# Inverse of the delta rule's triangular blocks: doubling block sizes on TensorE instead of substitution on VectorE

## The chip, the cores and the metric

One core of one Trainium2 chip runs the whole program. The metric is the device time of one execution in microseconds (us). TensorE (PE) multiplies matrices into PSUM, VectorE (DVE), ScalarE (ACT) and GpSimd (POOL) work beside it, and SyncE (SP) issues most of the DMAs.

## The reference, cut to what matters

Two transformer blocks follow each other over 1024 positions of width 1024. The second has, beside a state space model and an MLP, the delta rule of RWKV-7 with 8 heads of width 64:

```python
def step(state, inp):
    r_t, w_t, k_t, v_t, kk_t, b_t = inp
    sk = jnp.einsum('bhvk,bhk->bhv', state, kk_t)
    state = (state * w_t[:, :, None, :]
             - sk[..., None] * b_t[:, :, None, :]
             + v_t[..., None] * k_t[:, :, None, :])
    return state, jnp.einsum('bhvk,bhk->bhv', state, r_t)
```

The kernel does not step through 1024 positions. It takes them in chunks of 64, in which the steps become products of matrices; for that it needs, for each head and chunk, the inverse of a unit triangular 64x64 matrix. The change is about how that inverse is formed.

## The kernel before, in words

The 1024 positions are two halves (h = 0, 1) of four tiles of 128 positions; `rwkv(tt)` (L1226) does one tile, which is two chunks of 64 positions for 8 heads, so 16 triangular matrices. Chunk c lies on partitions 64c to 64c+63. The eight calls come from `sequences` (L923), four in a row per half, and the state links each tile to the next.

Within a tile: the masked products `MM` are made (L1328; `MM[:, h, c, 0]` holds the strictly triangular part); a block of 32x32 of each is copied to `ltc` (L1333), written to DRAM as `lt_d` (L1335, four DMAs) and read back as `L` (L1337, one DMA that repeats it over four groups of partitions), so that each partition holds a block of its own. Then VectorE substitutes in 31 steps of two instructions (L1387, L1389). The result `T` goes to DRAM as `tt_d` (L1391, four DMAs) and comes back as the diagonal blocks of `TT` (L1396, four DMAs). The off-diagonal 32x32 blocks take a transpose on VectorE (L1401), 16 small products (L1405), a copy on ScalarE (L1407), 16 more products (L1411) and two copies (L1415). `TT` is then used by L1422. The steps between L1339 and L1379 (transposes, `PQ`, `XV`, `TBK`, `W`, `G1`) don't need `TT`.

All matrix products of `rwkv` are float32 and show as two PE instructions each (16 products are x32). The large projections use split operands and three products each (`mm3`, L63; lines L66, L68, L69), one PE instruction of 512 columns each.

Order: each engine has a static order. A planner places the instructions when the kernel is built, by a model of their durations, with the order of the code as priority; steps under `urgent` come first. `sequences` writes the four tiles ahead of the projections `in2` of columns 1792 (h = 0) or 2304 (h = 1) to 4352 (L944), and the MLP follows: `ffn` of the first block's second half after h = 0 (L1090), seven of eight blocks of the second block's MLP after h = 1 (L1104). The planner puts these projections between the steps of the tiles. Their sums leave PSUM through VectorE (L902) or ScalarE (L881, L900, L1166), and their weights are loaded by SP, cast by ScalarE (L116) and split by GpSimd (L118). After h = 1, `merge_in` (L1776) reads what the tiles wrote.

The small products use the PSUM pool `tp` with four buffers in a ring; the projections use the pool `mm` with four.

Of the kernel before, what the change touches and what calls it, by code (L numbers as in the profile page):

```python
# [8 lines left out]
F32 = mybir.dt.float32  # L9
# [5 lines left out]
OP = mybir.AluOpType  # L15
# [4 lines left out]
S = 1024  # L20
D = 1024
HALF = 512
P = 128
# [11 lines left out]
class Kernel:  # L35
# [1134 lines left out]
    def rwkv_setup(self):  # L1170
        nc, I = self.nc, self.I
        c = self.rkc = self.pool("rkc")
        self.stp = self.pool("stp", 2)
        self.lora = c.tile([P, 512], F32, name="lora")
        nc.sync.dma_start(self.lora[0:64], I["w_decay_up_2"][0])
        nc.sync.dma_start(self.lora[64:128], I["w_aaa_up_2"][0])
        self.wgu = c.tile([P, 512], F32, name="wgu")
        nc.sync.dma_start(self.wgu, I["w_gate_up_2"][0])

        self.reset = c.tile([P, P], F32, name="reset")  # L1180
        nc.vector.memset(self.reset, 1.0)
        nc.vector.memset(self.reset.rearrange("p (c t) -> p c t", t=64)[:, :, 0:1], 0.0)

        self.mask2 = c.tile([P, 2, 64], F32, name="mask2")
        nc.gpsimd.memset(self.mask2, 1.0)
        for ch in range(2):
            q = self.mask2[64 * ch:64 * ch + 64]
            for m in range(2):
                nc.gpsimd.affine_select(q[:, m, :], q[:, m, :], pattern=[[1, 64]],
                                        compare_op=OP.is_gt if m == 0 else OP.is_ge, fill=0.0, base=0,  # L1190
                                        channel_multiplier=-1)

        self.ind = c.tile([P, 4, 8], F32, name="ind")
        nc.gpsimd.memset(self.ind, 0.0)
        self.blk = c.tile([P, P], F32, name="blk")
        nc.gpsimd.memset(self.blk, 0.0)
        for e in range(2):
            r = slice(64 * e, 64 * e + 64)
            nc.gpsimd.memset(self.blk[r, r], 1.0)
            for kt in range(4):  # L1200
                nc.gpsimd.memset(self.ind[r, kt, 2 * kt + e:2 * kt + e + 1], 1.0)

        self.eye2 = c.tile([P, 64], F32, name="eye2")
        nc.vector.tensor_copy(self.eye2[0:64], self.ident[0:64, 0:64])
        nc.vector.tensor_copy(self.eye2[64:128], self.ident[64:128, 64:128])

        self.eye32 = c.tile([P, 8, 32], F32, name="eye32")
        nc.gpsimd.memset(self.eye32, 0.0)
        for g in range(4):
            nc.gpsimd.affine_select(self.eye32[32 * g:32 * g + 32], self.eye32[32 * g:32 * g + 32],  # L1210
                                    pattern=[[-4, 8], [1, 32]], compare_op=OP.not_equal, fill=-1.0, base=-g,
                                    channel_multiplier=0)
        self.state = self.stp.tile([P, 4, 64], F32, name="state")
        nc.vector.memset(self.state, 0.0)
        self.lt_d = [self.dram.tile([32, 32, 32], F32, name=f"lt_d{t}") for t in range(8)]
        self.tt_d = [self.dram.tile([32, 8, 4, 32], F32, name=f"tt_d{t}") for t in range(8)]

    def rwkv_pools(self, st):
        self.rk = self.pool("rk", st=st)
        self.ew = self.pool("ew", 4, st=st)  # L1220
        self.TT = self.rk.tile([P, 8, P], F32, name="TT")
        self.nc.vector.memset(self.TT, 0.0)
        self.TI = self.rk.tile([P, 8, 32], F32, name="TI")
        self.nc.vector.memset(self.TI, 0.0)

    def rwkv(self, tt):  # L1226
        nc = self.nc
        rk = self.rk
        h, tok = tt // 4, slice(tt % 4 * P, tt % 4 * P + P)
        C = math.exp(-0.5)  # L1230
        V = nc.vector

        def big(name):
            return rk.tile([P, 4, P], F32, name=name)
# [10 lines left out]
        def ps512():  # L1245
            return self.tp.tile([P, 512], F32, name="tp")
# [7 lines left out]
        def pair(i):  # L1254
            return slice(64 * (i % 2), 64 * (i % 2) + 64), slice(i // 2 * 64, i // 2 * 64 + 64)

        chunks = [(c, slice(64 * c, 64 * c + 64)) for c in range(2)]
# [11 lines left out]
        for kt in range(4):  # L1269
            f = slice(kt * P, kt * P + P)  # L1270
            nc.tensor.matmul(pw[:, f], self.lora[0:64, f], zw[0:64, 0, :], start=True, stop=True)
            nc.tensor.matmul(pa[:, f], self.lora[64:128, f], zw[64:128, 0, :], start=True, stop=True)
        sg, a = big("sg"), big("a")
        for kt in range(4):
            f = slice(kt * P, kt * P + P)
            nc.scalar.activation(sg[:, kt, :], pw[:, f], AF.Sigmoid, bias=self.w0[:, kt:kt + 1])
        for kt in range(4):
            f = slice(kt * P, kt * P + P)
# [41 lines left out]
        MM = rk.tile([P, 8, 2, 2, 64], F32, name="MM")  # L1320
        for hh in range(0, 8, 2):
            for e in range(2):
                r = slice(64 * e, 64 * e + 64)
                ps = ps512()[:, :256].rearrange("p (c a i) -> p c a i", c=2, a=2)
# [2 lines left out]
                                     PR[r, :, hh // 2, 64 * c:64 * c + 64], start=True, stop=True)  # L1327
                V.tensor_tensor(MM[:, hh + e], ps, self.mask2[:, None].to_broadcast([P, 2, 2, 64]), op=OP.mult)  # L1328

        lt = rk.tile([P, 8, 32], F32, name="ltc")  # L1330
        for b in range(4):
            r = slice(32 * b, 32 * b + 32)
            V.tensor_copy(lt[r], MM[r, :, b // 2, 0, 32 * (b % 2):32 * (b % 2) + 32])  # L1333
        for b in range(4):
            nc.sync.dma_start(self.lt_d[tt][8 * b:8 * b + 8].rearrange("h j i -> j h i"), lt[32 * b:32 * b + 32])  # L1335
        L = rk.tile([P, 32, 32], F32, name="L")
        nc.sync.dma_start(L, self.lt_d[tt].rearrange("b j i -> b (j i)")[None].to_broadcast([4, 32, 1024]))  # L1337

        PQ = rk.tile([P, 8, 2, 64], F32, name="PQ")  # L1339
        XV = rk.tile([P, 2, 8, 64], F32, name="XV")  # L1340
# [1 line left out]
        ps = ps512()  # L1342
# [3 lines left out]
        ps = ps512()  # L1346
        for kt in range(4):
            self.transpose(ps[:, kt * P:kt * P + P], zv[:, kt, :])
        for c in range(2):
            r = slice(64 - 64 * c, 128 - 64 * c)  # L1350
            nc.scalar.copy(XV[r, c], ps[r].rearrange("p (h d) -> p h d", h=8))
        for c in range(2):
            ps = ps512()
# [6 lines left out]
        for i in range(8):  # L1360
            for c in range(2):
                r = slice(64 - 64 * c, 128 - 64 * c)
                nc.tensor.matmul(pq[64 * c:64 * c + 64, i * 64:i * 64 + 64], MM[r, i, c, 0, :], XV[r, c, i, :],
                                 start=True, stop=True)
# [4 lines left out]
        for kt in range(4):  # L1369
            f = slice(kt * P, kt * P + P)  # L1370
# [7 lines left out]
        V.tensor_tensor(W, W, k4(pg), op=OP.mult)  # L1378
        V.tensor_tensor(G1, k4(pg), bc(self.lnw), op=OP.mult)  # L1379

        T = rk.tile([P, 8, 32], F32, name="T")
        tmp = rk.tile([P, 8, 32], F32, name="Ttmp")
        nc.gpsimd.tensor_copy(T, self.eye32)
        for j in range(31):
            n = j // 4 + 1
            w = 31 - j
            V.tensor_tensor(tmp[:, :n, :w], L[:, j:j + 1, j + 1:].to_broadcast([P, n, w]),  # L1387
                            T[:, :n, j:j + 1].to_broadcast([P, n, w]), op=OP.mult)
            V.tensor_tensor(T[:, :n, j + 1:], T[:, :n, j + 1:], tmp[:, :n, :w], op=OP.subtract)  # L1389
        for cg in range(4):  # L1390
            nc.sync.dma_start(self.tt_d[tt][:, :, cg, :], T[32 * cg:32 * cg + 32])  # L1391
        TT, TI = self.TT, self.TI
        for c in range(2):
            nc.gpsimd.memset(TT[64 * c:64 * c + 32, :, 64 * c + 32:64 * c + 64], 0.0)
        for r in range(4):
            nc.sync.dma_start(TT[32 * r:32 * r + 32, :, 32 * r:32 * r + 32],  # L1396
                              self.tt_d[tt][8 * r:8 * r + 8].rearrange("h m g i -> (m g) h i"))

        for c in range(2):
            r = slice(64 * c, 64 * c + 32)  # L1400
            V.transpose(TI[r], TT[r, :, 64 * c:64 * c + 32])  # L1401
        pz = ps512()
        for i in range(8):
            for c, q in chunks:
                nc.tensor.matmul(pz[q, i * 32:i * 32 + 32], MM[q, i, c, 0, :], TI[q, i, :], start=True, stop=True)  # L1405
        Z = rk.tile([P, 8, 32], F32, name="Z")
        nc.scalar.copy(Z, pz[:, :256].rearrange("p (h j) -> p h j", h=8))  # L1407
        po = ps512()
        for i in range(8):
            for c, q in chunks:  # L1410
                nc.tensor.matmul(po[64 * c:64 * c + 32, i * 32:i * 32 + 32], Z[q, i, :], TT[q, i, 64 * c + 32:64 * c + 64],  # L1411
                                 start=True, stop=True)
        for c in range(2):
            r = slice(64 * c, 64 * c + 32)
            nc.scalar.copy(TT[r, :, 64 * c + 32:64 * c + 64], po[r, :256].rearrange("p (h i) -> p h i", h=8))  # L1415

        X = rk.tile([P, 8, 64], F32, name="X")
        for hg in range(2):
# [7 lines left out]
            for c in range(2):  # L1426
                q = slice(64 * c, 64 * c + 64)
# [5 lines left out]
        for i in range(8):  # L1433
            r, o = pair(i)
# [5 lines left out]
        for i in range(8):  # L1440
            r, o = pair(i)
# [6 lines left out]
        for c, q in chunks:  # L1448
            for i in range(8):
                r, o = pair(i)  # L1450
# [10 lines left out]
        for c, q in chunks:  # L1461
            for i in range(8):
                r, o = pair(i)
# [4 lines left out]
            pst = ps512()  # L1468
            for i in range(8):
                r = slice(64 * (i % 2), 64 * (i % 2) + 64)  # L1470
                nc.tensor.matmul(pst[r, i // 2 * 64:i // 2 * 64 + 64], FT[r, i // 2, q], self.state[r, i // 2, :],
                                 start=True, stop=True)
# [17 lines left out]
        r = self.rstd(var, 8, 1.0 / 64, 64e-5, rk)  # L1490
        V.tensor_tensor(y, y, r[:, :, None].to_broadcast([P, 8, 64]), op=OP.mult)
        po = ps512()
# [378 lines left out]
```

## Time and profile before

| what | value |
|---|---|
| median of 3 runs | 3047.42 us |
| lowest and highest of them | 3038.46, 3047.6 us |
| profiled execution, time | 3063.16 us |
| profiled execution, span of the records | 3061.4 us |
| PE busy in the span | 2831.0 us (92%) |
| DVE, ACT, POOL busy | 1745.7, 1245.3, 1460.9 us |
| the four tiles of h = 0 | about 1160 to 1655 us of the span |
| the four tiles of h = 1 | about 2010 to 2520 us of the span |

The profile gives busy time per engine, the waits of an engine with the instruction that ended them, a timeline of instructions, and the granted TensorE clock (1.00 is 2.4 GHz, 0.50 is 1.2 GHz). A group of PE instructions has its first start and a modelled length that overlaps the next group; the distance from its start to the start of the next one is what it occupies.

### The profile page before, as it was taken

How to read it: one execution, taken by the hardware profiler on the slowest of the kernel's cores; microseconds unless marked ns; L12 is line 12 of the kernel's file. 1: busy time of each engine (PE TensorE's matmuls, PEld its weight loads, DVE VectorE, ACT ScalarE, POOL GpSimd, SP SyncE). 2: the span in 40 equal slices, each digit the busy share in tenths (PEclk: the TensorE clock that was granted, in tenths of full speed). 3: DMA queues.
4: the chain of work that ended last, by engine and by line, in shares of the span. 5: the costliest groups of instructions: out<-in, count | busy, mean ns of one | idle time of the engine just before them, and what ended most of it. 6: DMA issues, size and time to landing. Idle time of an engine off the chain costs nothing.

```text
span 3061.4 us, 42378 instructions
## 1 busy us (share of the span) xinstructions
PE 2831.0 (92%) x15600; PEld 2337.1 (76%) x15600; DVE 1745.7 (57%) x3752; ACT 1245.3 (41%) x2121; POOL 1460.9 (48%) x1285
## 2 busy tenths in 40 slices
PE   6977998999998899889989999998899999999998
PEld 5865776787887777667777888887777778888887
DVE  5699569999946944445563563433655634332122
ACT  4545555444455333343333443332433333433333
POOL 4665544544445743434433465443343435454444
PEclk9988999999999999899999999999999999999999
DMA  7445332222224555333225484653323235442232
GB/s 252 136 130 178 124 118 64 90 79 69 73 84 148 179 164 152 103 86 90 76 84 147 147 274 123 178 147 107 81 92 90 82 90 155 141 131 97 97 97 83
DMA packets 301504, 370.22 MB, mean 121 GB/s; under 512 B 70936, under 2 KB 209902, under 8 KB 301040
## 3 DMA queue, kind: packets, MB, share of 16 engines
q1 hardware_dynamic: 293296, 351.75, 37.9%
q10 hardware_dynamic: 8000, 15.76, 1.5%
q8 instruction: 123, 2.02, 0.3%
q14 instruction: 85, 0.70, 0.1%
HBM read 315.80 MB, written 51.65 MB: 120 GB/s over the span
## 4 chain that ended last, share of the span: by engine, by line
PE 57%; DVE 27%; DMA 8%; issue 3%; ACT 2%; SPq 2%; POOL 1%; ACTq 0%; POOLq 0%; DVEq 0%
PE mm L66 16%; PE mm L68 16%; PE mm L69 16%; DVE junk L669 4%; DMA L<-lt_d 3%; DVE T L1389 2%; DVE Ttmp L1387 2%; DVE topk L680 2%; PE tp L128 1%; DVE acc L902 1%; DVE score L643 1%; DVE p L746 1%; DMA TT<-tt_d 1%; DVE p L735 1%; PE tp L764 1%
## 5 line engine op out<-in xcount | busy, mean ns | idle before, releaser
L118 POOL TENSOR_TENSOR whl<-wraw,whl 128x512 fp32r<-128x512 f32 (+1 forms) x836 | 1134.7, 1382 | 1255.7 <-ACT whl L116 1187.1
L66 PE MATMUL mm<-hT,whl 128*128 128x512 f32 x1760 | 699.1, 398 | 21.6 <-DVE acc L902 13.5
L68 PE MATMUL mm<-hT,whl 128*128 128x512 f32 x1760 | 701.6, 400 | 0.0
L69 PE MATMUL mm<-hT,whl 128*128 128x512 f32 x1760 | 694.8, 397 | 3.9 <-POOL whl L118 3.9
L116 ACT CAST whl<-wraw 128x1024 fp32r<-128x1024 f32 (+1 forms) x418 | 435.1, 1042 | 541.5 <-PE mm L69 389.7
L66 PE MATMUL mm<-whl,hT 128*128 128x512 f32 (+1 forms) x1584 | 614.6, 402 | 42.9 <-DVE acc L902 18.5
L68 PE MATMUL mm<-whl,hT 128*128 128x512 f32 (+1 forms) x1584 | 625.6, 396 | 0.4 <-POOL whl L118 0.4
L69 PE MATMUL mm<-whl,hT 128*128 128x512 f32 (+1 forms) x1584 | 614.3, 396 | 0.9 <-DVE hT L61 0.9
L66 PEld LDWEIGHTS mm<-hT,whl 128*128 128x128 f32 x1760 | 336.1, 191 | 97.2 <-DVE acc L902 15.2
L69 PEld LDWEIGHTS mm<-hT,whl 128*128 128x128 f32 x1760 | 336.3, 191 | 73.7 <-POOL whl L118 5.0
L66 PEld LDWEIGHTS mm<-whl,hT 128*128 128x128 f32 x1584 | 305.2, 193 | 112.2 <-DVE acc L902 22.2
L68 PEld LDWEIGHTS mm<-hT,whl 128*128 128x128 f32 x1760 | 336.1, 191 | 66.3 <-issue 0.9
L68 PEld LDWEIGHTS mm<-whl,hT 128*128 128x128 f32 x1584 | 305.9, 193 | 60.7 <-issue 1.2
L69 PEld LDWEIGHTS mm<-whl,hT 128*128 128x128 f32 x1584 | 303.3, 192 | 62.2 <-DVE hT L61 1.8
L902 DVE TENSOR_TENSOR acc<-mm,acc 128x512 f32<-128x512 f32 x240 | 160.6, 686 | 189.2 <-PE mm L69 188.7
L61 DVE TENSOR_TENSOR hT<-sm,hT 128x512 fp32r<-128x512 f32 x112 | 94.4, 846 | 265.2 <-ACT hT L60 264.5
L881 ACT ACTIVATE sm<-mm 128x512 f32<-128x512 f32 x128 | 76.5, 598 | 273.1 <-PE mm L69 267.3
L669 DVE TENSOR_SCALAR_CACHE_REDUCE junk<-score,topk 128x640 uint8<-128x640 f32 (+4 forms) x192 | 179.5, 941 | 1.8
L1387 DVE TENSOR_TENSOR Ttmp<-L,T 128x60 f32<-128x60 f32 (+24 forms) x248 | 77.8, 314 | 95.5 <-DMA L<-lt_d 88.1
L60 ACT CAST hT<-sm 128x512 fp32r<-128x512 f32 x144 | 89.3, 620 | 31.0 <-DVE sm L1835 28.3
L764 PE MATMUL tp<-pT,vhl 128*128 128x256 f32 x288 | 64.1, 310 | 25.0 <-ACT pT L760 7.4
L743 ACT ACTIVATE p<-p,nm 128x128 f32<-128x128 f32 (+7 forms) x64 | 49.6, 778 | 91.4 <-DVE nm L739 60.5
(470 smaller groups left out, 3489.2 us busy)
## 6 DMA issues: line engine op xcount, KB each, us to landing
wraw<-w_ff SPq DMA_DIRECT2D x128, 512.0 KB
wraw<-w_in SPq DMA_DIRECT2D x100, 512.0 KB
wraw<-w_ff_up SPq DMA_DIRECT2D x64, 512.0 KB
wraw<-w_ff_down SPq DMA_DIRECT2D x64, 512.0 KB
wraw<-w_ada SPq DMA_DIRECT2D x32, 512.0 KB
wraw<-w_out SPq DMA_DIRECT2D x32, 512.0 KB
raw<-w_ada SPq DMA_DIRECT2D x16, 512.0 KB
x_d<-acc ACTq DMA_DIRECT2D x16, 512.0 KB
```

The costliest lines, as they stand in the source:

```text
L60: self.nc.scalar.copy(hi, src)
L61: (engine or self.nc.gpsimd).tensor_tensor(lo, src, hi.bitcast(F32), op=OP.subtract)
L66: nc.tensor.matmul(ps, a[0], b[0], start=start, stop=False)
L68: nc.tensor.matmul(ps, a[0], b[1], start=False, stop=False)
L69: nc.tensor.matmul(ps, a[1], b[0], start=False, stop=stop)
L116: nc.scalar.copy(hl[:, 0], raw)
L118: nc.gpsimd.tensor_tensor(hl[:, 1, s], raw[:, s], hl[:, 0, s].bitcast(F32), op=OP.subtract)
L669: V.tensor_scalar(junk[:, :n], sel, value, 0.0, op0=op, op1=OP.add, accum_out=cnt)
L764: nc.tensor.matmul(o, self.vhl[(s0 + i) // 4][:, (s0 + i) % 4, kv, :], t[:, x, 256 * i:256 * i + 256], start=(s0 + i + x == 0), stop=(s0 + ...
L881: nc.scalar.activation(r, ps, AF.Relu)
L902: nc.vector.tensor_tensor(d, pss[j], d, op=OP.add)
L1387: V.tensor_tensor(tmp[:, :n, :w], L[:, j:j + 1, j + 1:].to_broadcast([P, n, w]), T[:, :n, j:j + 1].to_broadcast([P, n, w]), op=OP.mult)
```

## The change

Setup builds seven masks `joins` of 64x64 (six block patterns of width 2 to 64, and one of the neighbours above the diagonal) instead of `eye32`. In each tile, the copy to `ltc`, both trips through DRAM, the 62 instructions of the substitution, the transpose and the 32 products of 32 columns go. In their place: the identity is subtracted from the triangular blocks of `MM`, one group of 16 products of 64x64x64 (`each`) transposes them, masks start `S` and `St` at blocks of two, and five rounds double the block size. A round is a group of 16 products, a masked multiply on VectorE, two more groups (one in the last round) and two copies on ScalarE (in the last round two copies of half the partitions into `TT`).

```diff
@@ rwkv_setup
-        self.eye32 = c.tile([P, 8, 32], F32, name="eye32")
-        nc.gpsimd.memset(self.eye32, 0.0)
-        for g in range(4):
-            nc.gpsimd.affine_select(self.eye32[32 * g:32 * g + 32], self.eye32[32 * g:32 * g + 32],
-                                    pattern=[[-4, 8], [1, 32]], compare_op=OP.not_equal, fill=-1.0, base=-g,
-                                    channel_multiplier=0)
+        self.joins = c.tile([P, 7, 64], F32, name="joins")
+        nc.gpsimd.memset(self.joins, 0.0)
+        for ch in range(2):
+            q = self.joins[64 * ch:64 * ch + 64]
+            for x in range(6):
+                w = 1 << x
+                low = q[:, x].rearrange("p (b u) -> p b u", u=2 * w)[:, :, :w]
+                nc.gpsimd.memset(low, 1.0)
+                n = 32 // w
+                nc.gpsimd.affine_select(low, low, pattern=[[-2 * w, n], [0, w]], compare_op=OP.is_ge, fill=0.0, base=-w,
+                                        channel_multiplier=1)
+                nc.gpsimd.affine_select(low, low, pattern=[[2 * w, n], [0, w]], compare_op=OP.is_ge, fill=0.0,
+                                        base=2 * w - 1, channel_multiplier=-1)
+            up = q[:, 6].rearrange("p (b u) -> p b u", u=2)[:, :, 1:2]
+            nc.gpsimd.affine_select(up, up, pattern=[[-2, 32], [0, 1]], compare_op=OP.not_equal, fill=1.0, base=0,
+                                    channel_multiplier=1)
+        nc.vector.tensor_tensor(self.joins, self.joins, self.eye2[:, None].to_broadcast([P, 7, 64]), op=OP.add)
...
@@ rwkv, after MM
-        lt = rk.tile([P, 8, 32], F32, name="ltc")
-        for b in range(4):
-            r = slice(32 * b, 32 * b + 32)
-            V.tensor_copy(lt[r], MM[r, :, b // 2, 0, 32 * (b % 2):32 * (b % 2) + 32])
-        for b in range(4):
-            nc.sync.dma_start(self.lt_d[tt][8 * b:8 * b + 8].rearrange("h j i -> j h i"), lt[32 * b:32 * b + 32])
-        L = rk.tile([P, 32, 32], F32, name="L")
-        nc.sync.dma_start(L, self.lt_d[tt].rearrange("b j i -> b (j i)")[None].to_broadcast([4, 32, 1024]))
+        S, St, Y = (rk.tile([P, 8, 64], F32, name=n) for n in ("S", "St", "Y"))
+
+        def join(x):
+            return self.joins[:, x, None, :].to_broadcast([P, 8, 64])
+
+        def each(ps, a, b):
+
+            for i in range(8):
+                for c, q in chunks:
+                    nc.tensor.matmul(ps[q, i * 64:i * 64 + 64], a[c][q, i], b[q, i], start=True, stop=True)
+
+        M = [MM[:, :, c, 0, :] for c in range(2)]
+        eye = self.eye2[:, None, :].to_broadcast([P, 8, 64])
+        for c, q in chunks:
+            V.tensor_tensor(M[c][q], M[c][q], eye[q], op=OP.subtract)
+        for c, q in chunks:
+            V.tensor_tensor(St[q], M[c][q], join(6)[q], op=OP.mult)
+        ps = ps512()
+        each(ps, M, eye)
+        V.tensor_tensor(S, ps.rearrange("p (h d) -> p h d", h=8), join(0), op=OP.mult)
@@ rwkv, after W and G1
-        T = rk.tile([P, 8, 32], F32, name="T")
-        tmp = rk.tile([P, 8, 32], F32, name="Ttmp")
-        nc.gpsimd.tensor_copy(T, self.eye32)
-        for j in range(31):
-            n = j // 4 + 1
-            w = 31 - j
-            V.tensor_tensor(tmp[:, :n, :w], L[:, j:j + 1, j + 1:].to_broadcast([P, n, w]),
-                            T[:, :n, j:j + 1].to_broadcast([P, n, w]), op=OP.mult)
-            V.tensor_tensor(T[:, :n, j + 1:], T[:, :n, j + 1:], tmp[:, :n, :w], op=OP.subtract)
...
+        TT = self.TT
+        for x in range(1, 6):
+            ps = ps512()
+            each(ps, M, S)
+            V.tensor_tensor(Y, ps.rearrange("p (h d) -> p h d", h=8), join(x), op=OP.mult)
+            ps, pst = ps512(), ps512()
+            each(pst, (Y, Y), St)
+            pst = pst.rearrange("p (h d) -> p h d", h=8)
+            if x < 5:
+                each(ps, (St, St), Y)
+                nc.scalar.copy(S, ps.rearrange("p (h d) -> p h d", h=8))
+                nc.scalar.copy(St, pst)
+            else:
+                for c, q in chunks:
+                    nc.scalar.copy(TT[q, :, q], pst[q])
```

The lines left out of the second part are those from the DMAs to `tt_d` (L1390) to the copies into `TT` (L1415), which go with it; the two clears of `TT` on GpSimd (L1394) go too.

## Rows read from the trace of the kernel before

**Rows 1.** The page, part 1: busy time by engine, share of the span, instructions.
```profile
PE 2831.0 (92%) x15600; PEld 2337.1 (76%) x15600; DVE 1745.7 (57%) x3752; ACT 1245.3 (41%) x2121; POOL 1460.9 (48%) x1285
```

**Rows 2.** A window of one tile: busy PE, PEld, DVE, ACT, POOL; clock; DMA.
```profile
1282.00:1400.00 118.00, 107.00 (x762) 86.34 (x763) 61.50 (x137) 50.67 (x85) 46.33 (x38) 0.94 0.28 77
```

**Rows 3.** The chain that ended last, within the first tile: start us, us, what.
```profile
1194.25 1.43 DVE MM L1328 x4
...
1257.94 1.78 PE tp L1422 x16
```

**Rows 4.** Waits of PE, whole span: us in total, times, longest.
```profile
PE tp L1405 <- DVE TI L1401: 42.7, 8, 9.5
...
PE tp L1271 <- ACT zw L1266: 6.5, 1, 6.5
...
PE mm L66 <- ACT whl L116: 5.8, 4, 3.5
```

**Rows 5.** Waits of PE for L902, first in 1160 to 1660, then 2010 to 2520.
```profile
PE mm L66 <- DVE acc L902: 14.0, 2, 7.6
...
PE mm L66 <- DVE acc L902: 13.5, 3, 6.4
```

**Rows 6.** Timeline 1436 to 1466 (start, us, what, idle before): DVE twice, then PE.
```profile
1451.26 0.19 DVE L1387 TENSOR_TENSOR Ttmp<-L,T 128x31 f32<-128x31 f32 x1 [10.20 <-DMA L<-lt_d]
...
1457.31 0.68 DVE L902 TENSOR_TENSOR acc<-mm,acc 128x512 f32<-128x512 f32 x1
...
1458.05 0.79 PE L66 MATMUL mm<-whl,hT 128*128 128x512 f32 x1 [6.31 <-DVE acc L902]
```

**Rows 7.** Windows after the first gap, and the first and last of eight stretches.
```profile
1242.00:1245.00 3.00, 2.60 (x33) 2.44 (x34) 0.69 (x2) 0.28 (x1) 1.84 (x2) 0.50 0.86 271
...
1220.00:1260.00 40.00, 30.52 (x182) 25.03 (x182) 14.45 (x48) 9.58 (x15) 12.76 (x12) 0.83 0.45 133
...
2420.00:2480.00 60.00, 50.39 (x289) 40.56 (x287) 30.10 (x81) 16.77 (x26) 17.48 (x14) 0.89 0.31 86
```

**Rows 8.** Timeline of PE, 1608 to 1616: the two groups that go, and projections.
```profile
1608.36 1.49 PE L1405 MATMUL tp<-TI,MM 64*64 64x32 f32 x32 [1.47 <-DVE TI L1401]
1609.78 0.50 PE L66 MATMUL mm<-hT,whl 128*128 128x512 f32 x1
...
1614.77 0.70 PE L1411 MATMUL tp<-TT,Z 64*32 64x32 f32 x32
1615.39 0.50 PE L66 MATMUL mm<-hT,whl 128*128 128x512 f32 x1
```

**Rows 9.** Timeline of PE, 1203 to 1205.
```profile
1203.51 1.15 PE L1363 MATMUL tp<-XV,MM 64*64 64x64 f32 x32
1204.59 1.16 PE L1371 MATMUL tp<-zw,wgu 128*128 128x128 f32 x8
```

**Rows 10.** Timeline of PE, 1262 to 1265.
```profile
1262.98 0.39 PE L66 MATMUL mm<-hT,whl 128*128 128x512 f32 x1
1263.30 0.69 PE L1436 MATMUL tp<-MM,X 64*64 64x64 f32 x32
1263.82 0.65 PE L1443 MATMUL tp<-TBK,X 64*64 64x64 f32 x32
1264.39 0.50 PE L68 MATMUL mm<-hT,whl 128*128 128x512 f32 x1
1264.73 0.39 PE L69 MATMUL mm<-hT,whl 128*128 128x512 f32 x1
1264.96 0.40 PE L66 MATMUL mm<-hT,whl 128*128 128x512 f32 x1
```

**Rows 11.** A copy out of PSUM on ACT, 1160 to 1660: busy us, mean ns, idle before.
```profile
L1365 ACT COPY PQ<-tp 128x512 f32<-128x512 f32 x4 | 2.3, 586 | 13.0 <-PE tp L1363 13.0
```

**Rows 12.** The line of the old mask on POOL: ns min/median/max, starts.
```profile
L1210 POOL TENSOR_SCALAR_AFFINE_SELECT eye<-eye x4: 436/438/443, 981.9 to 983.3; 32x256 f32<-32x256 f32 x4
```

**Rows 13.** Groups by line on PE, 2010 to 2520 (one of six lines of projections).
```profile
L66 PE MATMUL mm<-hT,whl 128*128 128x512 f32 x342 | 138.4, 407 | 14.3 <-DVE acc L902 13.5 <-DVE hT L343 0.8
```

More of the change, by code (lines that the diff above doesn't have):

```diff
@@ L1205, in rwkv_setup @@
         nc.vector.tensor_copy(self.eye2[64:128], self.ident[64:128, 64:128])
-        self.eye32 = c.tile([P, 8, 32], F32, name="eye32")
-        nc.gpsimd.memset(self.eye32, 0.0)
-        for g in range(4):
-            nc.gpsimd.affine_select(self.eye32[32 * g:32 * g + 32], self.eye32[32 * g:32 * g + 32],
-                                    pattern=[[-4, 8], [1, 32]], compare_op=OP.not_equal, fill=-1.0, base=-g,
-                                    channel_multiplier=0)
+        self.joins = c.tile([P, 7, 64], F32, name="joins")
[15 more added lines that the diff above has]
+        nc.vector.tensor_tensor(self.joins, self.joins, self.eye2[:, None].to_broadcast([P, 7, 64]), op=OP.add)
         self.state = self.stp.tile([P, 4, 64], F32, name="state")
         nc.vector.memset(self.state, 0.0)
-        self.lt_d = [self.dram.tile([32, 32, 32], F32, name=f"lt_d{t}") for t in range(8)]
-        self.tt_d = [self.dram.tile([32, 8, 4, 32], F32, name=f"tt_d{t}") for t in range(8)]
     def rwkv_pools(self, st):
@@ L1222, in rwkv_pools @@
         self.nc.vector.memset(self.TT, 0.0)
-        self.TI = self.rk.tile([P, 8, 32], F32, name="TI")
-        self.nc.vector.memset(self.TI, 0.0)
     def rwkv(self, tt):
@@ L1390, in rwkv @@
[L1390 to L1412, printed above, removed]
@@ L1413, in rwkv @@
-        for c in range(2):
-            r = slice(64 * c, 64 * c + 32)
-            nc.scalar.copy(TT[r, :, 64 * c + 32:64 * c + 64], po[r, :256].rearrange("p (h i) -> p h i", h=8))
+        TT = self.TT
[13 more added lines that the diff above has]
+                    nc.scalar.copy(TT[q, :, q], pst[q])
```

## The prediction, made before the changed kernel was run

> **What bounds the kernel now.** I read the page first, then windows of about a tile each. PE is busy for 2831.0 us, 92% of the span [rows 1], and also while the tiles of the delta rule run: 107.00 of 118 us in the second one, for example [rows 2]. Projections that don't depend on the tile fill PE between its steps, so the chain of a tile (62 us from the end of the masks at 1195.68 to L1422 at 1257.94 [rows 3]) is mostly covered. What a tile costs is therefore PE's own work, PE's gaps, and time at the low clock. So I count these three.
>
> The waits of PE come next. Eight times, once per tile, PE stands at L1405 until the blocks are back from DRAM: 42.7 us in all [rows 4]. Five more gaps inside the tiles wait for L902, an addition on DVE that has nothing to do with the delta rule: 14.0 + 13.5 = 27.5 us [rows 5]. The timeline shows why. DVE stood 10.20 us at the first substitution, waiting for the DMA of L, with L902 behind it in its queue; L902 came at 1457.31, and PE went on 0.74 us later after 6.31 us idle [rows 6]. The same picture, DVE at L1387 and then L902, precedes the other four. By contrast the other hand-overs of a tile (PE to DVE or ACT and back, about twelve per tile) cost PE almost nothing: over all eight tiles L1271 with 6.5 us is the largest [rows 4].
>
> Third, the clock. In the first gap the granted clock fell to 0.50, and it was still there when PE worked again, 2.60 of 3 us from 1242 to 1245 [rows 7]. A level of 0.50 is 1.2 GHz, 1.00 is 2.4 GHz.
>
> **The change, part by part.** The sum is made against the profiled execution, 3063.16 us, which is 15.7 us (0.5%) above the median of 3047.42.
>
> *Added on PE.* A tile gets 1 group of 16 products at the start, 3 in each of four rounds and 2 in the last: 15, so 120 in eight tiles. The price of a group is the term that decides. L1363 has the same 16 products of 64x64x64, alternating between two diagonally opposite quarters of the array, and occupies 1204.59 - 1203.51 = 1.08 us [rows 9]. L1436, with the same shapes and count over four quarters, occupies 0.52 us [rows 10]. L1405 runs over the same two quarters as the new groups with half the columns and occupies 1.42 us, partly because its second chunk came late [rows 8]. The new code alternates chunk 0 (rows and columns 0 to 63) with chunk 1 (64 to 127), as L1363 alternates two; I take 1.08 and keep 0.52 and 1.42 as ends. 120 x 1.08 = +129.6 us (62 to 170).
>
> L1405 has half the moving columns of L1363 but is not faster [rows 8, 9], so the loading of weights seems to set the pace. The Trainium skill, page "TensorE: Matmul & The Clock Gate", section "LDWEIGHTS (loading the stationary operand)", prices a load by its columns alone, 64/1.2 = 53 ns here; an estimate from it, 32 loads one after the other, is 1.7 us per group, 205 us for 120, and the sum would end near +107 us instead of mine. The trace disagrees with that use of the rule: 1.08 us for 32 products is 34 ns each, so the loads of two quarters overlap.
>
> *Entering and leaving.* Between projections of 0.23 us each (1264.96 - 1264.73), L1436 starts 0.09 us late (1262.98 + 0.23 = 1263.21, start 1263.30), and the first projection behind the groups takes 0.34 instead of 0.23 us, 0.11 more [rows 10]. That is 0.2 us per insertion. A tile has 11 insertions (start, two per round) instead of 2 (L1405, L1411): 9 x 0.2 x 8 = +14.4 us (0, if groups stand next to other small products, to 25 at twice the price).
>
> *Removed on PE.* L1405 at 1.42 and L1411 at 0.62 us [rows 8]: 8 x 2.04 = -16.3 us.
>
> *Gaps.* With no DMA in the chain, the gaps at L1405 and behind the substitution go: -42.7 - 27.5 = -70.2 us. What is late next is the new chain's own hand-overs, 11 a tile, 88 in all. I cost them at nothing, because the twelve of the same kind cost nothing [rows 4]: the projections cover them. If the cover is thin, half a microsecond each would be 44 us.
>
> *Clock.* Eight stretches, one per tile, hold these gaps. In the first, 40 us at 0.83 lose 40 x 0.17 = 6.8 us; in the last 60 x 0.11 = 6.6 [rows 7]; the eight add to 46.4. A part of that fell while PE stood idle and is already counted; windows of 2 us over the tiles put 29.5 us on working time outside the first tile's start. -29.5 us (20 to 40).
>
> *VectorE.* The 62 steps of a tile go, and 4 copies. Ten instructions of about 0.68 us come (two subtractions, two masks for St, six masked multiplies out of PSUM, of L902's size) [rows 6]: 6.8 us. DVE gets emptier. The new wait on DVE is for a group of products; L902 and the splits of projections are queued behind it. PE comes to such groups in the planned order, as it does to L1363 or L1422 now, whose evacuations hold up no projection [rows 4, 5]. Zero.
>
> *ScalarE.* Ten copies of 0.59 us [rows 11], 5.9 us a tile, against three shorter ones that go. ACT is busy for 50.67 of 118 us in a tile [rows 2]; PE waits for them only if the fill is short. Zero, inside the hand-overs above.
>
> *DMAs and SP.* 13 DMAs a tile go from SP's queue, with their waits; weight loads stood behind them. In the whole span PE waits only 5.8 us for weights that ACT casts [rows 4], so zero. *PSUM:* 16 turns of the ring of four instead of 2; each buffer is freed by the very step for which the chain waits. Zero.
>
> *Setup.* POOL gets 12 small clears, 26 selections and a clear instead of five instructions. The old selections took 0.44 us each [rows 12]. At 0.2 to 0.4 us each some 9 us more on POOL; half of it I put on the path: +4 us (0 to 9).
>
> Sum: 129.6 + 14.4 - 16.3 - 70.2 - 29.5 + 4 = +32 us. 3063 becomes 3095 in a profiled execution, the median 3047.4 becomes 3079, given as **3080**.
>
> *Is there still enough fill?* Before, 1601 projections lay in 2010 to 2520 (342, 342, 341 and three times 192; the first of the six lines in [rows 13]). By the code, 384 of in2 and 1344 of seven MLP blocks are to be had: 1728, or 393 us at 0.23. A hand-over takes about 5 us now (L1405 ended 1609.78, L1411 began 1614.77 [rows 8]). The new chain is then 3 us of DVE, 15 groups (16 us) and 11 x 5 = 55 us: 74 instead of 62 us, so a tile grows by some 12 us. Of the 510 us of that stretch 364 were projections (1601 x 0.2275), 35 gaps and 15 low clock (half of the sums above); 96 are left, 24 a tile for its own products, 40 with 16 more. A tile then lasts 127.5 + 12 and takes 99.5 us of fill, four take 398 against 393. It suffices, barely.
>
> **The rivals.**
>
> *A. The groups run at the four-quarter rate.* If products of neighbouring groups and the two chunks overlap as in L1436, a group costs 0.52 us: 120 x 0.56 = 67 us less, +32 becomes -35, 3012 us. It decides from 0.81 us per group downward (32/120 = 0.27 below 1.08). For it: the shapes and the count are those of L1436 and L1443 [rows 10]. Against: L1363 and L1405, which use two quarters as the new groups do [rows 8, 9]. Chance 0.15.
>
> *B. The chain becomes the bound.* If a hand-over takes 6 us, the chain is 3 + 16 + 66 = 85 us and a tile lasts 127.5 + 23 = 150.5 us. Less 40 us of its own, four tiles want 442 us of fill, and h = 1 has 393. PE then idles 49 us: +81, 3128 us. It decides from the 5 us on. For it: before L1365 ACT idled 13.0 us in four tiles [rows 11], so engines do wait in turn. Against: 5 us is what the row shows. Chance 0.15.
>
> *C. Thin cover.* Half a microsecond at each of 88 hand-overs, or the L902 gaps stay because DVE now waits for products instead of a DMA: +28 to +44 on top, near 3120 us. Against: the near-zero waits at the present hand-overs [rows 4]. Chance 0.2.
>
> *D. The loads of weights queue up.* At L1405's rate a group costs 1.42 us: 41 us more, +73, 3120 us. For it: L1405 is the one row on the very same quarters [rows 8]. Against: L1363 [rows 9]. Chance 0.05. The page's rule on LDWEIGHTS points this way.
>
> My forecast has 0.45, with its own range of 3050 to 3105 from the ends of entering, clock and setup.
>
> **How the numbers follow.** 0.3%, 9 us, is about what a measurement of this kernel can tell from no change. Faster by more: all of A and a little of the forecast's lower end, 0.2. Within: 0.1. Slower: 0.7. The range takes B in and cuts most of A off: 3020 to 3145.
>
> **What would show it.** The group lines of the new products should be spaced by about 1.08 us per x32; PE's waits at the old L1405 and at L902 within tiles should be gone, and the granted clock in the tiles near 1.00; PE's busy time should rise although the clock does, and DVE's should fall. The forecast is wrong if the groups are far from 1.08 us, if new waits of PE for the masked multiply or the copies add up to over 20 us, or if PE idles at the end of h = 1 before `merge_in`'s products.

## The result and the profile after

The changed kernel takes 3143.26 us (median of 4 runs) against 3047.51 us: ratio 1.0322, interval 1.0301 to 1.0343. The profiled execution took 3143.37 us, 80.2 us more than that of before (3063.16, which lay 15.7 us above its median; by the medians the difference is 95.8). The direction was forecast, with +32 us the size was not.

The page of the changed kernel, span and part 1, answers to [rows 1]:

```profile
span 3141.7 us, 48480 instructions
PE 2939.0 (94%) x18928; PEld 2431.4 (77%) x18928; DVE 1617.1 (51%) x3287; ACT 1281.6 (41%) x2177; POOL 1467.9 (47%) x1295
```

PE is busy for 108 us more; its idle time falls from 3061.4 - 2831.0 = 230.4 to 202.7 us, 28 less. 108 - 28 = 80: this accounts for the whole difference of the two profiles. All records of the new products together (their one line in the code; PE, then PEld, then the clock):

```profile
0.00:3141.70 3141.70, 133.12 (x3840) 120.09 (x3840) 0.96 0.37 116
```

133.1 us for 120 groups, 1.11 each (these modelled lengths overlap what follows; a group occupies 1.07, as shown below). The forecast had 129.6.

Windows of the changed kernel: both stretches of tiles, the stretch right behind the first, and the one around the end of the second (its last tile ends at 2616).

```profile
1160.00:1720.00 560.00, 558.29 (x5085) 457.07 (x5086) 207.06 (x334) 223.26 (x355) 219.69 (x164) 0.99 0.29 87
2080.00:2600.00 520.00, 518.77 (x4735) 423.56 (x4736) 190.18 (x312) 200.03 (x314) 198.41 (x148) 1.00 0.28 86
...
1720.00:1850.00 130.00, 84.67 (x475) 73.68 (x474) 55.30 (x48) 34.20 (x59) 45.84 (x33) 0.74 0.66 188
2600.00:2640.00 40.00, 24.51 (x252) 19.98 (x251) 17.45 (x29) 14.06 (x21) 7.24 (x6) 0.79 0.33 99
```

Within the tiles PE is now busy for 558.29 of 560 and 518.77 of 520 us at a clock of 0.99 and 1.00; compare [rows 2]. The gaps of [rows 4, 5] are gone. But at the end of each half there is a hole: 45.3 us idle at the first, 15.5 at the second, at clocks of 0.74 and 0.79. In the kernel before, the stretches behind the halves had 8.8 and 1.2 us idle:

```profile
1655.00:1790.00 135.00, 126.16 (x713) 105.78 (x712) 64.96 (x65) 57.42 (x91) 65.73 (x50) 0.97 0.70 204
...
2520.00:2640.00 120.00, 118.76 (x522) 97.40 (x521) 53.41 (x62) 46.33 (x61) 61.29 (x44) 1.00 0.52 166
```

PE's two longest waits in the changed kernel name what it stood for. L1753 is a copy of the state space model, whose first products come right behind the tiles of h = 0 in every kernel here. L1789 is the first copy of `merge_in`: in h = 0 it waits for what the state space model writes (14.2 us of PE), in h = 1 it comes behind the last tile's output (8.3 us).

```profile
PE mm L66 <- ACT hT L1789: 22.5, 2, 14.2
PE tp L1767 <- POOL s5t L1753: 21.7, 1, 21.7
```

What ran out are the projections. Their records alone (those that read weights `whl`; PE busy, count, clock), before and then changed: within the four tiles of h = 0, and from there to the first copy of `merge_in`; at the end, the same for h = 1 of the changed kernel:

```profile
1190.00:1651.00 461.00, 344.91 (x1408) 0.95 0.31 89
1651.00:1747.00 96.00, 70.39 (x297) 0.96 0.65 174
...
1185.00:1711.00 526.00, 396.48 (x1654) 1.00 0.27 82
1711.00:1816.00 105.00, 30.82 (x133) 0.69 0.63 169
...
2100.00:2616.00 516.00, 379.42 (x1581) 1.00 0.27 83
2616.00:2623.00 7.00, 0.00 (x0) 0.50 0.60 187
```

The longer tiles of h = 0 took 246 projections more, and 133 instead of 297 were left to cover the state space model. In h = 1 none were left, against 41 before.

The tiles end later because each lasts longer: in h = 0 the last instruction of successive tiles stands 138 us apart (1297.83, 1435.87, 1573.78, 1711.32), before 121. The chain of the first tile, from the end of the masks to the product with `TT` (L1422 before, L1423 now), was 62 us [rows 3] and is 78:

```profile
1188.89 1.42 DVE L1336 TENSOR_TENSOR MM<-tp,mask 128x256 f32<-128x256 f32 x4 [2.74 <-PE tp L1334]
...
1268.16 1.06 PE L1423 MATMUL tp<-PQ,TT 128*128 128x128 f32 x8
```

Over the eight tiles it grew from 64 to 81 us on average. The timeline of one half of a round shows what a hand-over is made of (PE, with the masked multiply on DVE from its own timeline):

```profile
1219.10 1.15 PE L1348 MATMUL tp<-S,MM 64*64 64x64 f32 x32
1220.17 0.50 PE L69 MATMUL mm<-hT,whl 128*128 128x512 f32 x1
...
1225.07 0.39 PE L69 MATMUL mm<-hT,whl 128*128 128x512 f32 x1
1225.39 1.15 PE L1348 MATMUL tp<-St,Y 64*64 64x64 f32 x32
...
1220.29 0.69 DVE L1406 TENSOR_TENSOR Y<-tp,joins 128x512 f32<-128x512 f32 x1 [11.60 <-PE tp L1348]
```

The group occupies 1.07 us. The multiply has ended at 1220.98, yet the next group comes at 1225.39: the planner has put 22 projections between, 5.2 us. PE loses nothing by that at once, but those projections are spent, and the chain is 5.2 us longer. Nearly every hand-over inside the rounds has this length; the first two of a tile take 8.5 and 5.5 us.

### The profile page after: what moved, and what is told of

It reads as the page before. It is cut to its first block, busy times and chain, and to the rows that moved or that the text cites. A ratio compares the mean times of both kernels' runs of the same rounds, so it can differ in the third digit from the quotient of the medians.

```text
span 3141.7 us, 48480 instructions
## 1 busy us (share of the span) xinstructions
PE 2939.0 (94%) x18928; PEld 2431.4 (77%) x18928; DVE 1617.1 (51%) x3287; ACT 1281.6 (41%) x2177; POOL 1467.9 (47%) x1295
## 5 line engine op out<-in xcount | busy, mean ns | idle before, releaser
L902 DVE TENSOR_TENSOR acc<-mm,acc 128x512 f32<-128x512 f32 x240 | 160.9, 687 | 248.7 <-PE mm L69 248.4
L1406 DVE TENSOR_TENSOR Y<-tp,joins 128x512 f32<-128x512 f32 x40 | 27.6, 690 | 177.3 <-PE tp L1348 177.3
```

What stands on the lines that cost most here:

```text
L902: nc.vector.tensor_tensor(d, pss[j], d, op=OP.add)
```

## The experiments

Two theories stood against each other. F: the new products cost PE what was forecast, and on top of it the longer chain of a tile uses up the projections, so that PE idles at the end of each half (the mechanism of rival B in the prediction). W: only PE's added work slows the kernel, and the holes have another cause. Each ratio is to the kernel before, run beside it. The code is cut; "..." marks what is left out.

**e_powers.** The same number of groups, fewer hand-overs: the inverse as a product of powers of the strictly triangular block. A stage squares `A` and its transpose `At`, and multiplies the result `R` with the factor `AI` of the stage before, side by side.

```diff
-        for x in range(1, 6):
...
+        a, at = M, (At, At)
+        for x in range(1, 7):
+            if x < 6:
+                pt = ps512()
+                each(pt, a, at)
+            if x < 5:
+                pa = ps512()
+                each(pa, at, a)
+            if x > 1:
+                pr = ps512()
+                each(pr, (AI, AI), (R, R))
...
```

> The inverse as a product of powers, (I - U)(I + U^2)(I + U^4) up to U^32, in place of the doubling of block sizes: again 15 groups of 16 products per tile on the same two quarters of the array, but only 7 places in the chain where PE waits for an evacuation, instead of 11. Theory F (the chain of a tile grew from 62 to 79 us, so the projections run out and PE idles after each half): 4 hand-overs of some 6.5 us less make the chain about 53 us, the idle time and low clock after the halves (some 60 us idle) go, and the time falls from 3143 to about 3070 us. Rival W (the slowdown is PE's added work, 133 us of groups, and the idle after the halves has another cause): only 4 insertions of 0.2 us per tile are saved, 3137 us.

3063.76 us, ratio 1.0047 (1.0029 to 1.0065). F's number; W is off by 73 us. A tile of h = 1 lasts 109 us (last instructions at 2132.14, 2239.73, 2351.52, 2457.63), and the holes are closed, as the windows behind its tiles show (those of h = 0 end at 1596):

```profile
1596.00:1746.00 150.00, 141.63 (x780) 119.15 (x779) 51.88 (x55) 49.48 (x74) 67.72 (x46) 0.97 0.53 153
2457.00:2577.00 120.00, 119.97 (x528) 98.70 (x527) 38.49 (x46) 46.70 (x59) 60.07 (x44) 1.00 0.40 127
```

**e_quarters.** The same powers; odd heads cross to the other half of the columns in every stage, and each half of the rows writes a PSUM bank of its own.

```diff
...
+            pss = [ps512().rearrange("p (g k d) -> p g k d", g=2, k=4) for b in range(2)]
+            for k in range(4):
+                for g, (a, b) in enumerate(groups):
+                    for e in range(2):
+                        for c in range(2):
+                            i = c if s % 2 == 0 else c ^ e
+                            nc.tensor.matmul(pss[i][half[i ^ e], g, k], at(a, s, c, e, k), at(b, s, c, e, k), start=True,
+                                             stop=True)
...
```

> The same product of powers, with the products of odd heads crossing to the other half of the columns in every stage, so that all four quarters of the array work as in L1436: a full-rate group costs 0.52 us instead of 1.08, and a tile has about 9 us of groups instead of 16.2. Theory F with PE as the bound once the chain is short: 7.3 us x 8 = 58 us below the same powers on two quarters, about 3010 us, which is below the kernel before (3047). Rival W: work alone counts, 58 + 6 us below the changed kernel, 3079 us. If four quarters give nothing with a shared bank of PSUM: as the powers on two quarters.

3023.58 us, ratio 0.9922 (0.9893 to 0.995): 0.8% below the kernel before. The products of its stages took 74.84 us, its transposing group, still on two quarters, 9.19. A stage in its timeline shows the rate: on four quarters two groups in 0.98 us, the third in 0.58.

```profile
1215.43 1.16 PE L1341 MATMUL tp<-XA 64*64 64x64 f32 x64
1216.41 0.65 PE L1341 MATMUL tp<-R,AI 64*64 64x64 f32 x32
1216.99 0.50 PE L66 MATMUL mm<-hT,whl 128*128 128x512 f32 x1
```

Against the 124.04 us of e_powers that saves 40 us, not the 58 expected, and the medians differ by 40: within the noise, work on PE comes out one to one here.

**e_copy.** One more copy in the chain of the changed kernel.

```diff
             V.tensor_tensor(Y, ps.rearrange("p (h d) -> p h d", h=8), join(x), op=OP.mult)
+            V.tensor_copy(Y2, Y)
...
```

> The changed kernel with one more copy on VectorE in each round, between the masked multiply and the products that read it: no work on PE is added, the chain of a tile gets 5 x 0.7 us longer by the copy's own time, more if the planner leaves more room. Theory F: the projections have run out already, so the longer chain comes out one to one: 8 x 3.5 to 8 x 7 us, +28 to +56, 3171 to 3199 us. Rival W: no work on PE, so no change, 3143 us.

3151.84 us, ratio 1.0333 (1.0302 to 1.0364), not to be told from the changed kernel's 1.0322. This is W's number, a miss of F: the tiles of h = 0 ended at 1730.9 instead of 1711.3, but PE idled about as long in 1720 to 1860 (45 us against 46). Of the 20 us only 7 came out at the first copy of `merge_in`, since the way from the last tile to it took 92 us instead of 104, with 65 projections in it instead of 133. Why PE did not idle longer there is open; p_long below asks the same question with a larger step.

**e_rounds.** The rounds for x = 3 and 4 left out.

```diff
-        for x in range(1, 6):
+        for x in (1, 2, 5):
```

> The changed kernel with two of the five rounds left out (blocks of 8 and of 16 are not joined, so the inverse is not complete): 6 groups and 4 insertions per tile less on PE, (6 x 1.08 + 0.8) x 8 = 58 us, and 4 hand-overs less in the chain. Theory F: PE's work goes and the idle time after the halves with it: 58 + about 60 us, 3025 us. Rival W: 58 us, 3085 us.

3019.46 us, ratio 0.9904 (0.9867 to 0.9941). F's number again. Between the profiled executions (110 us; by the medians 124) PE's busy time fell by 58.5 us (2939.0 to 2880.5), as both theories had it; the other 52 us are idle time. This run shortens work and chain together, so it does not part them by itself.

**b_onchip.** What the two trips through DRAM cost the kernel before.

```diff
-            nc.sync.dma_start(self.lt_d[tt][8 * b:8 * b + 8].rearrange("h j i -> j h i"), lt[32 * b:32 * b + 32])
...
-        nc.sync.dma_start(L, self.lt_d[tt].rearrange("b j i -> b (j i)")[None].to_broadcast([4, 32, 1024]))
+        for x in range(2):
+            V.tensor_scalar(L[:, 16 * x:16 * x + 16].rearrange("p a b -> p (a b)").rearrange("p (h i) -> p h i", h=8), MM[:, :, x, 0, :], 0.01, None, op0=OP.mult)
...
+            V.tensor_scalar(TT[32 * r:32 * r + 32, :, 32 * r:32 * r + 32], T[32 * r:32 * r + 32], 0.001, None, op0=OP.mult)
...
```

> The kernel before with its substitution and its small products kept, but both trips through DRAM taken out: the block for the substitution is filled by two scaled copies of the masked products on VectorE, and the result goes into the diagonal blocks by four scaled copies. The blocks are not the right ones (no re-ordering of partitions, small factors keep the numbers finite), so this leaves the inverse out and keeps only the order and the amount of work. Forecast's terms (42.7 us at L1405, 27.5 us at L902 and 29.5 us of low clock are all due to the two waits for DMA): about 100 us less, 2948 us, PE's waits for L902 and at L1405 inside the tiles near zero. Rival (the planner's hand-overs put new waits in their place, or VectorE's 62 steps keep L902 waiting): half of it or less, about 3000 us, with L902 still among PE's waits.

2961.86 us, ratio 0.969 (0.9666 to 0.9714): 95 us of 3053 by the ratio, 91 by the medians (the kernel before had 3053.11 beside it), against a forecast of 100 for gaps and clock together. PE's waits in its stretch of tiles, 1160 to 2520, show what is left of 42.7 and 27.5 us:

```profile
PE tp L1395 <- DVE TI L1391: 4.8, 3, 2.2
PE mm L66 <- DVE acc L902: 4.0, 2, 3.0
```

**p_copy, p_long.** e_powers with copies in its chain, 8 and 36 a tile, and no work on PE.

```diff
-                V.tensor_copy(A, h8(pa))
+                V.tensor_copy(A1, h8(pa))
+                for n in range(4):
+                    V.tensor_copy(A2, A1)
+                    V.tensor_copy(A1, A2)
+                V.tensor_copy(A, A1)
```

This is p_long; p_copy has `A1`, `A2`, `A` once each.

> The product of powers on two quarters, with two more copies on VectorE in each of four stages, one behind the other, in the chain of the tile: no work on PE is added, the chain gets 4 x 2 x 0.7 = 5.6 us longer or more. Theory F (a longer chain costs nothing until the projections run out, and there they last beyond the end of the tiles): no change, 3064 us within 9 us. Rival (the length of the chain is on the path at any length): 8 x 5.6 = 45 us more, 3109 us.

p_copy: 3052.84 us, ratio 0.9997 (0.9985 to 1.0009). A tile lasts 113 to 119 us, and nothing is lost; it is even half a per cent below e_powers, more than the 9 us that were allowed for.

> The product of powers on two quarters (15 groups per tile, as the changed kernel has) with nine more copies on VectorE in each of four stages, one behind the other: 36 copies of 0.7 us per tile, no work on PE. With 8 copies a tile grew from 106 to 114 us and nothing was lost; with 36 it should last about 140 us, as in the changed kernel (138). Theory F (free until the projections run out, which is somewhere between 114 and 138 us a tile): PE idles after each half again, some 50 us and low clock behind it, and the time comes near the changed kernel's: 3053 + 50 to 80 us, 3103 to 3133 us. Rival (the doubling of block sizes loses time in another way than by the length of its chain): no change, 3053 us.

p_long: 3111.78 us, ratio 1.0198 (1.0176 to 1.022). A tile lasts 129 to 135 us (about 140 was expected), and the holes are back, for the same operands of `merge_in`:

```profile
1700.00:1850.00 150.00, 117.66 (x624) 99.04 (x624) 63.20 (x64) 48.23 (x78) 49.34 (x45) 0.83 0.65 197
2580.00:2680.00 100.00, 87.33 (x370) 70.98 (x371) 43.51 (x51) 32.83 (x40) 42.76 (x31) 0.91 0.51 163
...
PE mm L66 <- ACT hT L1782: 16.5, 1, 16.5
PE mm L66 <- DMA yin<-y_d: 8.2, 1, 8.2
```

The projections for h = 0 end early again (records as above, p_copy and then p_long):

```profile
1180.00:1617.00 437.00, 310.37 (x1283) 1.00 0.26 80
1617.00:1739.00 122.00, 104.02 (x423) 0.97 0.64 172
...
1182.00:1690.00 508.00, 377.91 (x1588) 1.00 0.27 83
1690.00:1795.00 105.00, 49.20 (x198) 0.79 0.71 202
```

The copies also load VectorE (1773.2 us busy against 1653.5), but that is not what holds PE: within the tiles of h = 0 it idled 4.4 us against 2.2. So with PE's work held fixed, the length of the chain costs nothing at about 115 us a tile and 59 us at about 132. This is what decides for F.

**p_twice.** One group of e_powers issued twice in four stages.

```diff
...
                 each(pa, at, a)
+                each(pa, at, a)
...
```

> The product of powers on two quarters, with the group for the untransposed power issued twice in four stages: 4 groups per tile more on PE, 32 groups of 1.08 us, the same hand-overs. Theory F (PE is the bound, so work on it comes out one to one): +35 us, 3098 us. Rival (there is slack on PE within the tiles, the hand-overs set the pace): less than 10 us.

3081.60 us, ratio 1.0086 (1.0065 to 1.0108). 35 us more were expected for the 32 groups; PE's busy time rose by 31 us over p_copy:

```profile
PE 2942.6 (96%) x19952; PEld 2448.5 (79%) x19952; DVE 1625.0 (53%) x3294; ACT 1288.6 (42%) x2185; POOL 1450.9 (47%) x1256
```

Of these 27 us show against p_copy (1.0086 - 0.9997 of 3053), but only 12 against e_powers (1.0047, from another chip). That work on PE is on the path is supported; one to one is not shown by this run, since p_copy, with more in its chain, is itself half a per cent below e_powers. Each edit makes the planner order thousands of instructions anew; that this alone moves the kernel by some 10 us would explain it, but was not tried.

**q_direct.** e_quarters with the transposed block from a product of its own.

```diff
+                    nc.tensor.matmul(pu[e][q, k], PR[r, 0, k, 64 * c:64 * c + 64], BK[r, k, 3 * c, :], start=True, stop=True)
```

> The product of powers on four quarters, where the transposed blocks come from a product of their own (operands swapped, over four quarters, with a mask for the lower triangle) instead of a transposition of the masked block: the first group costs 0.52 instead of 1.08 us and one hand-over goes. Theory F: 8 x 0.56 = 4.5 us less work on PE, the shorter chain is worth nothing: 0.9922 of the kernel before becomes about 0.9907, hardly to be told apart. Rival (the chain still counts): 8 x 5 us less, 0.979.

3015.87 us, ratio 0.9881 (0.9866 to 0.9896). The best version with a complete inverse: about 37 us below the kernel before and 4% below the changed one. F's 0.9907 lies just above its interval, within the reach of the two intervals together; the rival's 0.979 is excluded.

## Why the prediction was right in its direction and wrong in its size

*The price of a group* was right: 1.08 us taken, 1.07 in the timeline, 1.11 over all. Rivals A and D fall with it: the groups of the change use two quarters only, at the rate of L1363 [rows 9]. (D's 1.42 us is not the rate of those quarters: in b_onchip the group of L1405 occupies 1.05 us in half of the tiles.) The Trainium skill, page "TensorE: Matmul & The Clock Gate", section "LDWEIGHTS (loading the stationary operand)", was weighed ahead of the result: an estimate from its 53 ns per load, taken one after the other, made 205 us. The trace disagrees with that again, with 133.1 us. That rival A's rate of 0.5 us a group could be had by another order of the products was shown by e_quarters. The Trainium skill, page "TensorEngine Tiling (Array Packing)", section "Tile-to-Partition Mapping", lists four tiles in the 64x64 mode; the trace agrees, with 0.98 us for two groups over all four where one group over two took 1.07.

*Gaps and clock* were right for the tiles: 100 us forecast for both waits, 95 shown by b_onchip, where only six scaled copies on VectorE replaced the trips. That L902 was held up by the trips is shown by the same run; that it was the wait for L and not the second trip is read from [rows 6].

*PE's busy time* rose by 108 us where the terms (129.6 + 14.4 - 16.3 - 29.5) gave 98. Low clock in the new holes, which no term had, is in the difference: from 1760 to 1820 PE was busy for 29.59 us at 0.50, which costs 15.

```profile
1760.00:1820.00 60.00, 29.59 (x128) 28.43 (x129) 22.19 (x20) 13.27 (x25) 14.23 (x14) 0.50 0.53 154
```

*The hand-overs* were right in the rounds: 5 us taken, 5.2 measured, and no waits of PE at them while the projections lasted (rival C falls). But the start of a tile was sized too short, with 8.5 us for its first hand-over and one more ahead of the first group: the chain is 81 us, not 74, and a tile grew by about 17 us, not 12. That 139.5 us were forecast for a tile and 138 measured is luck: the base of 127.5 (510 / 4) was too long, as the tiles of before stood 121 us (h = 0) and 124 us (h = 1) apart.

*The step that failed* is "Is there still enough fill?", with its "It suffices, barely". It compared 398 us of wanted projections with 393 to be had, for the four tiles alone and for h = 1 alone; by these numbers 5 us were lacking already, and the tiles grew by more than it took. Above all, it left out that projections are also wanted behind the tiles: the state space model after h = 0 and `merge_in` after h = 1 each come behind the last tile, and need cover of their own. Before, the tiles of h = 0 ended at 1651 with 297 projections left for what followed; in the changed kernel they ended at 1711 with 133 left, and PE stood from 1752 on. h = 0, which the forecast did not count at all, has three quarters of the idle time (45.3 of 60.8 us). The kernel before already had 10 us idle in those stretches, so some 51 us are new, in the mechanism that rival B described. That B's 49 us come so close is luck: B put them all into h = 1 and took 6 us a hand-over. B had 0.15; with the tail counted it would have been the likeliest case.

The forecast's 32 and these 51 us make 83, near the 80 between the profiles, but that is not the whole sum: the 15 us of low clock come on top, and so other terms were too dear by some 18 us. Part of that is seen in the setup; where the rest lies is open.

The setup's selections on GpSimd were put at 4 us. No wait of PE names them, and the first tile's masks end at 1190.31 us, against 1195.68 before [rows 3]: the term does not show.

## What to carry to other kernels

Where one engine is full and independent work covers a long chain, that work is a stock: add up what the whole chain wants, and what must be covered behind it, before a chain is made longer. Trading a wait for work on the full engine pays only if the work is cheaper than the wait (here 133 us and their insertions against 95). In these kernels the order of the small products over the quarters of the array decided that price by a factor of two (1.07 us a group against 0.49). Of two algorithms with the same number of products, the one with fewer dependent stages was better here by some 80 us, because the other one used up the stock.

## What was not expected

A hand-over of 5.2 us came back in round after round, though the masked multiply took 0.69 us and was done 4.4 us before PE took its result: its length is the planner's. The waits for 13 small DMAs a tile were worth 95 us, 3%: PE's own wait for the blocks, the additions held up behind VectorE's wait, and the low clock after both. And the chain's length had no price at first: 8 more copies a tile cost nothing, 36 cost 59 us. Past that it was not one to one either, as e_copy shows.
